# Last phase of a streaming encoder layer: the work on a tile's inputs given out at the end of a step

## The chip, the cores and the metric

The kernel runs on one core of one Trainium2 chip. The metric is the device time of one execution in microseconds (us). Before the change it is 2288.26 us, the median of three runs (2287.53 to 2289.09).

The core has five engines that each work through their own list of instructions in order: TensorE (PE in the profile; PEld is its loading of weights), VectorE (DVE), ScalarE (ACT), GpSimd (POOL), and SyncE (SP), which in this kernel issues the transfers. An instruction that waits holds back all that stand behind it on its engine.

## The reference, cut to what matters

One layer of an encoder with two token mixers side by side (differential attention A and stick-breaking attention B) is applied to 2048 new frames and to 8 running streams of 16 frames with 512 cached positions each. The phase that the change touches computes the end of the layer:

```
oa = rms_norm(oa, subln_g) * (1.0 - lam_init)
ya = (oa.reshape(b, s, WIDTH_A) * jax.nn.silu(za)) @ w_branch_a
yb = (ob.reshape(b, s, WIDTH_B) * jax.nn.silu(zb)) @ w_branch_b
y  = (jax.nn.sigmoid(ga) * ya + jax.nn.sigmoid(gb) * yb) @ w_out
x  = x + gate * y
out = rms_norm(x, final_g)
```

The widths are 512 for each branch and 1024 for the model. `oa` and `ob` together make the 1024 columns called o, `za` and `zb` those called z, `ga` and `gb` the 2048 columns of gates.

## The kernel before, in words

The rows are cut into 17 tiles of 128: 16 of the prompt, and one that holds all 8 x 16 rows of the running streams. The earlier phases project the inputs and compute both attentions, and leave o, z and gates of each tile in DRAM (`o_d`, `z_d`, `g_d`). The last phase takes the tiles in the order 0 to 14, then the tile of the running streams, then tile 15. All matrix products are made from numbers split in two 16-bit halves (`split`, lines 287 to 292): high by high, high by low, low by high.

For each tile the last phase does this:

- `inputs` (lines 1215 to 1246) loads o (L1218), z (L1219) and two halves of the gates (L1223). It makes u = o x z x sigmoid(z), scaled by the norm of each head for branch A: the sigmoid on ScalarE into a PSUM bank named "mm" (L1229, which shows in the profile as L120, the line of the helper `act`), o x z on GpSimd (L1230), and the product with the bank on VectorE (L1232 and four times L1236). It applies the sigmoid to the gates in place (L1238, again L120), takes the sum of squares of u (L274), and splits u into `u16`.
- `turned` (L1251) turns u16 by a transposing DMA, so that it can stand as weights of a matrix product.
- `branches` makes four pieces (two halves of columns for each of two branches) of 12 products of 128x128 by 128x512 each (L1262) into a bank "mm"; VectorE multiplies each with its gate (L1264), GpSimd adds the two branches (L1266). After the fourth, `finish` squares y and splits it into `y16`.
- `turned_y` (L1287) turns y16 by a transposing DMA.
- `output` makes two halves of 24 products each (L1399) into a bank "o", multiplies them with the gate of the layer (L1403; L1405 and L1406 for the running streams), adds x on GpSimd (L1407), and after the second half takes the norm of the row (L274, L255 to L266), scales it (L1412) and stores it (L1413). x is loaded at the first half (L1392).

Buffers: o, z and u16 have one buffer each (`hs`), the gates two tiles' worth, the turned u two, the turned y and y16 one. The banks "mm" and "o" are two each; "s" has three and "t" one.

The phase runs in steps n = 0 to 17 (L1439 to L1452). Step n makes the branches of the n-th tile in order, the output of the one before, and the inputs of the one two ahead. The list `work` of a step holds, in this order: two pieces of branches, the turn of u for the next tile, two pieces of branches, the inputs of tile n+2, two pieces of output of tile n-1, the turn of y of tile n. `interleave` spreads the steps of a second list (`aside`) through it: the attention of the running streams over their caches (`sample`; it loads caches at L753 and L758, transposes them at L777 and copies them at L778, and runs through steps 0 to 12), called the sample lane here. For the first two tiles `inputs` is called before this phase, in `early_work`.

The order of this list is a priority, not the final order: a scheduler places the instructions on each engine by their readiness in its own estimate of times, and gives out the banks in that order. A manual dependency of the kind NOSYNC orders two instructions of one engine without a wait. `act` uses it to keep the instructions that need an activation table in the order written.

Of the kernel before, what the change touches and what calls it, by code (L numbers as in the profile page):

```python
# [21 lines left out]
ALU = mybir.AluOpType  # L22
# [10 lines left out]
NT = SEQ // P  # L33
# [77 lines left out]
def layer_kernel(ctx: ExitStack, tc: tile.TileContext, a: dict):  # L111
    nc = tc.nc
    V, S, G, T = nc.vector, nc.scalar, nc.gpsimd, nc.tensor
# [1092 lines left out]
    L = {}  # L1206
# [5 lines left out]
        split(dst[:, 0, :, :], dst[:, 1, :, :], st, s, S if n % 2 else G)  # L1212
        return dst

    def inputs(t):

        o, z = hs[0:2]
        load(out=o, in_=o_d[t])  # L1218
        load(out=z, in_=z_d[t])  # L1219
        gs = []  # L1220
        for j in range(2):
            gs.append(L["g"][(2 * len(begun) + j) % 4].rearrange("p (b n) -> p b n", b=2))
            load(out=gs[j], in_=g_d[t].rearrange("p (b n) -> p b n", b=2)[:, :, j * 512 : (j + 1) * 512])  # L1223
        begun.append(t)
        r = L["orms"][:, 4 * t : 4 * t + 4] if t < NT else rsqrt(osums[:, NT, :], 4, P, tiny, "rA")
        for n in range(2):
            c = slice(n * 512, (n + 1) * 512)
            sg = bank("mm")
            act(out=sg, in_=z[:, c], func=AF.Sigmoid)  # L1229
            G.tensor_tensor(out=o[:, c], in0=o[:, c], in1=z[:, c], op=ALU.mult)  # L1230
            if n == 1:
                V.tensor_tensor(out=o[:, c], in0=o[:, c], in1=sg, op=ALU.mult)  # L1232
            else:
                for h in range(4):
                    c = slice(h * P, (h + 1) * P)
                    V.scalar_tensor_tensor(out=o[:, c], in0=sg[:, c], scalar=r[:, h : h + 1], in1=o[:, c], op0=ALU.mult, op1=ALU.mult)  # L1236
        for g in gs:
            act(out=g, in_=g, func=AF.Sigmoid)  # L1238
        acc = tiny.tile([P, 1], F32, tag="uacc", name="uacc")
        sum_squares(o, D, acc)  # L1240
        su = scales(acc, unit, "su")
        u16 = hs[2].bitcast(F16).rearrange("p (f n) -> p f n", f=2)
        split(u16[:, 0, :], u16[:, 1, :], o, su[:, 0:1], S)
        iu = unit.tile([P, 1], F32, tag="iu", name="iu")
        V.tensor_tensor(out=iu, in0=su[:, 1:2], in1=L["s"][0][:, 1:2], op=ALU.mult)
        return dict(u16=u16, u=L["u"][len(begun) % 2], iu=iu, g=gs)

    def turned(st):

        st["u"] = st["u"].bitcast(F16).rearrange("p (k n) -> p k n", n=P)  # L1250
        nc.sync.dma_start_transpose(out=st["u"], in_=st["u16"].rearrange("p f n -> p (f n)"))  # L1251
# [33 lines left out]
    def turned_y(st):  # L1285
        st["y"] = yT = L["y"].bitcast(F16).rearrange("p (k n) -> p k n", n=P)
        nc.sync.dma_start_transpose(out=yT, in_=st["y16"].rearrange("p f n -> p (f n)"))  # L1287
# [18 lines left out]
    def early_work():  # L1306


        free.extend(units[7]["bufs"])

        def first(t):
            if "orms" not in L:
                L["orms"] = rsqrt(osums[:, 0:NT, :].rearrange("p t h -> p (t h)"), 4 * NT, P, con, "orms")
            states[t] = inputs(t)
            if t == tiles[0]:
                turned(states[t])

        def early(i):

            if i == 0:  # L1320
                L["first"] = [fn for _, fn in branches(states[tiles[0]])] + [lambda: turned_y(states[tiles[0]])]
            L["first"][i]()

        def rest():
            L["g"], L["u"], (L["y"], L["y16"]) = free[0:4], free[4:6], free[6:8]

        return [branch_weight for _ in branch_weights] + [rest] + [lambda t=t: first(t) for t in tiles[0:2]] \
            + [lambda i=i: early(i) for i in range(5)]
# [31 lines left out]
    with ExitStack() as c2:  # L1360
        def pool2(name, bufs):
            return c2.enter_context(tc.tile_pool(name=name, bufs=bufs, reuse_waits="tile"))

        dec = pool2("dec", 1)
        res = pool2("res", 1)
        s2 = pool2("s2", 2)
        wb, (s_b, s_o) = L["wb"], L["s"]
        wo = []
        for j in range(2):
            for k in range(0, KT, 2):  # L1370
                st = s2.tile([P, D], F32, tag="x", name="x", bufs=2)
                wo.append(cut(res.tile([P, 2048], F16, name=f"wo{len(wo)}"), st, w_out, k, j, s_o[:, 0:1], k // 2))
        gate = res.tile([P, D], F32, name="gate")
        sel = res.tile([16, 256], F32, name="sel")
        load(out=sel, in_=a["shapes"][0:16, C_SEL : C_SEL + 256])
        fg = gts

        def gate_rows(i, n):

            pg = bank("t")  # L1380
            gsm = s2.tile([P, 512], F32, tag="sg", name="gsm", bufs=2)
            load(out=gsm[0:9, :], in_=gate_d[:, n * 512 : (n + 1) * 512])
            T.matmul(pg, sel[0:9, i * P : (i + 1) * P], gsm[0:9, :], start=True, stop=True)
            return pg

        def output(t, st):
            box = {}

            def half(j):
                if j == 0:  # L1390
                    box["x"] = s2.tile([P, D], F32, tag="x", name="x2", bufs=2)
                    load(out=box["x"], in_=x_rows(t))  # L1392
                x = box["x"]
                c = slice(j * 512, (j + 1) * 512)
                po = bank("o")
                n = 0
                for yi, wi in ((0, 0), (0, 1), (1, 0)):
                    for k in range(KT):
                        T.matmul(po, st["y"][:, yi * 8 + k, :], wo[j * 4 + k // 2][:, wi, k % 2, :], start=(n == 0), stop=(n == 3 * KT - 1))  # L1399
                        n += 1  # L1400
                m = s2.tile([P, 512], F32, tag="sg", name="m", bufs=2)
                if t < NT:
                    V.scalar_tensor_tensor(out=m, in0=po, scalar=st["iy"], in1=gate[:, c], op0=ALU.mult, op1=ALU.mult)  # L1403
                else:
                    S.activation(out=m, in_=po, func=AF.Identity, scale=st["iy"])  # L1405
                    V.tensor_tensor(out=m, in0=m, in1=gate_rows(1, j), op=ALU.mult)  # L1406
                G.tensor_tensor(out=x[:, c], in0=m, in1=x[:, c], op=ALU.add)  # L1407
                if j == 1:
                    acc = tiny.tile([P, 1], F32, tag="facc", name="facc")
                    sum_squares(x, D, acc)  # L1410
                    r = rsqrt_one(acc, D, tiny, "rF")
                    V.scalar_tensor_tensor(out=x, in0=x, scalar=r, in1=fg, op0=ALU.mult, op1=ALU.mult)  # L1412
                    load(out=y_rows(t), in_=x)  # L1413

            return [(5.2, lambda j=j: half(j)) for j in range(2)]

        fixed = [res.tile([P, NB, 32], F32, name="qz"), res.tile([P, 2, P], F32, name="qn"), res.tile([P, P], F32, name="kn"),
                 [res.tile([P, 4, NB, 32], F32, name=f"wz{c}") for c in range(2)], res.tile([P, 2, P], F32, name="wn")]
        for x in fixed[0:2] + fixed[3]:
            G.memset(x, 0.0)  # L1420

        lane = []
        for u in range(8):
            for i, pieces in enumerate(sample(units[u], dec, fixed)):
                if S_PERIOD * u + i == len(lane):
                    lane.append([])
                lane[S_PERIOD * u + i] += pieces

        def aside(n):

            m = -(-len(lane) // max(1, S_TILES - n))
            made = [piece for pieces in lane[:m] for piece in pieces]
            del lane[:m]
            return made

        for n in range(2):
            S.copy(out=gate[:, n * 512 : (n + 1) * 512], in_=gate_rows(0, n))
        load(out=fg, in_=a["final_g"].rearrange("(o d) -> o d", o=1).to_broadcast([P, D]))
        for n in range(NT + 2):  # L1439
            work = []  # L1440
            if 0 < n <= NT:
                work += branches(states[tiles[n]])
            if n + 1 <= NT:

                work.insert(2, (0.9, lambda n=n: turned(states[tiles[n + 1]])))
            if n + 2 <= NT:
                work.insert(5, (0.1, lambda n=n: states.update({tiles[n + 2]: inputs(tiles[n + 2])})))
            if n > 0:
                work += output(tiles[n - 1], states.pop(tiles[n - 1]))
            if 0 < n <= NT:  # L1450
                work.append((0.9, lambda n=n: turned_y(states[tiles[n]])))
            interleave(work, aside(n))  # L1452


# [25 lines left out]
```

## Time and profile before

| | us |
|---|---|
| median of the runs | 2288.26 |
| the profiled execution | 2285.48 |
| its span | 2283.7 |
| TensorE busy over the span | 2085.1 (91%) |
| VectorE busy | 1611.5 (71%) |
| ScalarE busy | 1482.6 (65%) |
| GpSimd busy | 688.1 (30%) |

The first output products (L1399) of the last phase start at 1790.6 us and the last at 2272.8 us. A line of the timeline gives start and length in us, the engine, the line of the kernel, the operation, what it writes and reads, the number of instructions merged, and in brackets the idle time of the engine before it with what ended it. The chain of waits gives start, length and what. A line of the busy time by stretches gives the stretch, its length, then busy time and number of instructions of PE, PEld, DVE, ACT and POOL, the granted TensorE clock as a share of the full one, the busy share of the DMA engines, and GB/s. A line of the table of waits gives who waited for whom: total us, times, longest. `hs` is the buffers of o, z and u16; `wa` and `wb` are buffers of many uses, here gates, turned u and y; `ps_mm`, `ps_o`, `ps_s`, `ps_t` are the banks.

### The profile page before, as it was taken

Reading aid. Unit: us, or ns where it says so; the run is one execution under the profiler, and the core shown is the slowest. Engines: PE = TensorE matmul, PEld = TensorE weight load, DVE = VectorE, ACT = ScalarE, POOL = GpSimd, SP = SyncE. Lnnn points to the kernel's source line nnn. Section 1 sums busy time; section 2 is a strip of 40 time slices with the busy share of each in tenths; the row PEclk is TensorE's granted clock in tenths of the full one; section 3 lists DMA queues with packets and bytes.
Section 4 is the critical chain, followed back from the end, with each engine's and each line's share of the span. In section 5 each row is a group of like instructions: output and inputs, shape, how many; then the busy total and the mean of one; then the engine's idle time right before and its main releaser. Section 6 shows DMA issues by size and latency. Waiting matters only on the chain. (4 is left out here: it accounts for less than half of the span.)

```text
span 2283.7 us, 40470 instructions
## 1 busy us (share of the span) xinstructions
PE 2085.1 (91%) x14478; PEld 1110.4 (49%) x14478; DVE 1611.5 (71%) x3507; ACT 1482.6 (65%) x2952; POOL 688.1 (30%) x559
## 2 busy tenths in 40 slices
PE   4997999999999999899999989999986799888997
PEld 2554554555555455455545555555543444444443
DVE  4668767789875778987577898776777656565554
ACT  3877677787876777786677777666776544444431
POOL 1522012355301335530032553012344232232321
PEclk7999999999999999999999999999997899999998
DMA  8667658697875778876566886757687989788652
GB/s 295 211 212 187 163 131 220 148 221 155 206 169 124 170 154 199 177 179 131 128 172 142 204 183 154 153 140 163 151 179 173 295 228 262 202 220 211 188 150 65
DMA packets 763754, 411.92 MB, mean 180 GB/s; under 512 B 524986, under 2 KB 708586, under 8 KB 763040
## 3 DMA queue, kind: packets, MB, share of 16 engines
q1 hardware_dynamic: 762474, 408.86, 72.6%
q8 instruction: 113, 1.85, 0.3%
q14 instruction: 89, 0.73, 0.1%
q10 hardware_dynamic: 1078, 0.48, 0.1%
HBM read 211.53 MB, written 72.91 MB: 125 GB/s over the span
## 5 line engine op out<-in xcount | busy, mean ns | idle before, releaser
L423 PE MATMUL ps_mm<-wb,hs 128*128 128x512 f16 x1836 | 460.7, 382 | 0.6 <-DVE v L292 0.5
L629 POOL TENSOR_TENSOR sc_p<-sc_p,sc_n 128x1024 f32<-128x1024 f32 (+8 forms) x160 | 278.1, 1742 | 459.2 <-DVE sc_n L607 451.6
L423 PEld LDWEIGHTS <-hs 128*128 128x128 f16 x2928 | 256.1, 98 | 226.9 <-issue 6.8
L607 DVE TENSOR_TENSOR_SCAN sc_n<-ps_s,sc_n,zero_t 128x512 f32<-128x512 f32 x192 | 245.3, 1278 | 64.4 <-ACT ps_s L120 62.2
L423 PE MATMUL ps_mm<-wa,hs 128*128 128x512 f16 x1092 | 279.4, 380 | 0.0
L647 PE MATMUL ps_s<-k,qst 128*128 128x512 f16 (+3 forms) x640 | 225.9, 354 | 38.3 <-DVE sc_n L607 30.1
L120 ACT ACTIVATE sc_p<-ps_s,usc 128x512 f32<-128x512 f32 (+3 forms) x320 | 202.0, 631 | 85.8 <-PE ps_s L648 55.1
L495 PE MATMUL ps_mm<-wa,hs 128*128 128x512 f16 x1020 | 257.0, 379 | 0.0
L562 DVE TENSOR_TENSOR sc_n<-sc_p,sc_n 128x1024 f16<-128x1024 f32 (+7 forms) x160 | 197.9, 1242 | 41.3 <-ACT sc_n L561 41.2
L648 PE MATMUL ps_s<-k,qst 128*128 128x512 f16 (+3 forms) x640 | 226.2, 354 | 0.0
L1399 PE MATMUL ps_o<-wo,wb 128*128 128x512 f16 x816 | 199.5, 401 | 24.7 <-DMA wb<-wa 22.0
L706 PE MATMUL ps_o<-v,wt 128*128 128x128 f16 x1008 | 175.6, 226 | 27.6 <-DMA wt<-sc_n 27.5
L495 PEld LDWEIGHTS <-hs 128*128 128x128 f16 x1632 | 140.2, 98 | 119.0
L120 ACT ACTIVATE ps_s<-ps_s,usc 128x512 f32<-128x512 f32 (+3 forms) x320 | 193.7, 605 | 0.0
L561 ACT CAST sc_n<-sc_p 128x1024 f16<-128x1024 f32 (+7 forms) x160 | 138.5, 870 | 49.2 <-POOL sc_p L629 49.1
L707 PE MATMUL ps_o<-v,wt 128*128 128x64 f16 x1008 | 158.5, 198 | 0.0
L495 PE MATMUL ps_mm<-wb,hs 128*128 128x512 f16 x612 | 155.9, 379 | 0.0
L706 PEld LDWEIGHTS <-wt 128*128 128x128 f16 x1008 | 99.2, 102 | 102.7 <-DMA wt<-sc_n 38.0
L1399 PEld LDWEIGHTS <-wb 128*128 128x128 f16 x816 | 82.1, 102 | 130.4 <-DMA wb<-wa 26.1
L457 POOL TENSOR_TENSOR rot<-pr,rope 128x256 f32<-128x256 f32 x68 | 63.1, 928 | 247.1 <-ACT pr L437 193.3
L437 ACT ACTIVATE pr<-ps_mm,usc 128x512 f32<-128x512 f32 (+1 forms) x136 | 86.5, 636 | 67.4 <-PE ps_mm L423 67.1
L545 DVE TENSOR_SCALAR_CACHE_REDUCE sc_n<-ps_s,usc 128x512 f32<-128x512 f32 (+3 forms) x148 | 99.0, 669 | 42.4 <-PE ps_s L648 28.2
(336 smaller groups left out, 4346.7 us busy)
## 6 DMA issues: line engine op xcount, KB each, us to landing
hs<-hT_d SPq DMA_DIRECT2D x122, 512.0 KB, 4.2
g_d<-gt SPq DMA_DIRECT2D x68, 256.0 KB, 3.4
out_dram<-pr SPq DMA_DIRECT2D x204, 64.0 KB, 1.8
wa<-g_d SPq DMA_DIRECT2D x25, 512.0 KB, 6.7
wide<-in_w_ada_dram SPq DMA_DIRECT2D x12, 1024.0 KB, 8.4
wa<-in_w_in_dram SPq DMA_DIRECT2D x44, 256.0 KB, 4.7
z_d<-pr SPq DMA_DIRECT2D x136, 64.0 KB, 2.7
o_d<-o SPq DMA_DIRECT2D x136, 64.0 KB, 2.7
```

The lines of the kernel that those rows point to most:

```text
L120: i = S.activation(**kw)
L423: T.matmul(box["p"], box["h"][:, hi, k, :], U["w"][k][:, wi, :], start=(n == 0), stop=(n == 3 * KT - 1))
L495: T.matmul(box["g"][:, 0:gw], box["h"][:, hi, k, :], U["wg"][k // per][:, k % per, wi, :], start=(j == 0), stop=(j == 3 * KT - 1))
L561: S.copy(out=hi, in_=src)
L562: V.tensor_tensor(out=lo, in0=src, in1=hi, op=ALU.subtract)
L607: V.tensor_tensor_scan(out=dst[:, lo : lo + n][:, ::-1], data0=src[:, 0:n][:, ::-1], data1=zero_t[:, 0:1].to_broadcast([P, n]), initial=fi ...
L629: G.tensor_tensor(out=p[:, 0:m], in0=p[:, 0:m], in1=n[:, 1 : m + 1], op=ALU.mult)
L647: T.matmul(p[:, 0:n], qst[:, c, :], kk[:, c, 0:n], start=True, stop=False)
L648: T.matmul(p[:, 0:n], qst[:, 2 + c, :], kk[:, c, 0:n], start=False, stop=not diag)
L706: T.matmul(po[:, c * P : (c + 1) * P], wt[:, wj, :], vt[:, c, :, :], start=first, stop=False)
L707: T.matmul(po[:, c * P : c * P + 64], wt[:, nb + wj, :], vt[:, c, 0, :], start=False, stop=last)
L1399: T.matmul(po, st["y"][:, yi * 8 + k, :], wo[j * 4 + k // 2][:, wi, k % 2, :], start=(n == 0), stop=(n == 3 * KT - 1))
```

## The change

`inputs` is cut in two. `started` does the loads and picks the buffers; it stands in the list where `inputs` stood. The rest, still called `inputs`, moves to the end of the step, behind the output pieces and the turn of y. Its product on GpSimd is ordered behind the last addition of x that was written before it (`L["added"]`), and its four products on VectorE behind the last scaling of x (`L["scaled"]`), both without a wait. The turn of u moves from between the second and third piece of branches to behind the fourth. The calls before the phase do both parts one after the other, as before.

```diff
-    def inputs(t):
+    def started(t):
 
         o, z = hs[0:2]
         load(out=o, in_=o_d[t])
...
         begun.append(t)
+        return dict(t=t, g=gs, u=L["u"][len(begun) % 2])
+
+    def inputs(st):
+
+        t, gs = st["t"], st["g"]
+        o, z = hs[0:2]
         r = L["orms"][:, 4 * t : 4 * t + 4] if t < NT else rsqrt(osums[:, NT, :], 4, P, tiny, "rA")
         for n in range(2):
             c = slice(n * 512, (n + 1) * 512)
             sg = bank("mm")
             act(out=sg, in_=z[:, c], func=AF.Sigmoid)
-            G.tensor_tensor(out=o[:, c], in0=o[:, c], in1=z[:, c], op=ALU.mult)
+            i = G.tensor_tensor(out=o[:, c], in0=o[:, c], in1=z[:, c], op=ALU.mult)
+            if "added" in L:
+                tc.add_manual_dep(i.ins, L["added"].ins.name, NOSYNC, reason="order of tiles")
             if n == 1:
                 V.tensor_tensor(out=o[:, c], in0=o[:, c], in1=sg, op=ALU.mult)
             else:
                 for h in range(4):
                     c = slice(h * P, (h + 1) * P)
-                    V.scalar_tensor_tensor(out=o[:, c], in0=sg[:, c], scalar=r[:, h : h + 1], in1=o[:, c], op0=ALU.mult, op1=ALU.mult)
+                    i = V.scalar_tensor_tensor(out=o[:, c], in0=sg[:, c], scalar=r[:, h : h + 1], in1=o[:, c], op0=ALU.mult, op1=ALU.mult)
+                    if "scaled" in L:
+                        tc.add_manual_dep(i.ins, L["scaled"].ins.name, NOSYNC, reason="order of tiles")
         for g in gs:
             act(out=g, in_=g, func=AF.Sigmoid)
...
-        return dict(u16=u16, u=L["u"][len(begun) % 2], iu=iu, g=gs)
+        st.update(u16=u16, iu=iu)
...
-            states[t] = inputs(t)
+            states[t] = started(t)
+            inputs(states[t])
...
-                G.tensor_tensor(out=x[:, c], in0=m, in1=x[:, c], op=ALU.add)
+                L["added"] = G.tensor_tensor(out=x[:, c], in0=m, in1=x[:, c], op=ALU.add)
...
-                    V.scalar_tensor_tensor(out=x, in0=x, scalar=r, in1=fg, op0=ALU.mult, op1=ALU.mult)
+                    L["scaled"] = V.scalar_tensor_tensor(out=x, in0=x, scalar=r, in1=fg, op0=ALU.mult, op1=ALU.mult)
...
             if n + 1 <= NT:
 
-                work.insert(2, (0.9, lambda n=n: turned(states[tiles[n + 1]])))
+                work.append((0.9, lambda n=n: turned(states[tiles[n + 1]])))
             if n + 2 <= NT:
-                work.insert(5, (0.1, lambda n=n: states.update({tiles[n + 2]: inputs(tiles[n + 2])})))
+                work.append((0.1, lambda n=n: states.update({tiles[n + 2]: started(tiles[n + 2])})))
             if n > 0:
                 work += output(tiles[n - 1], states.pop(tiles[n - 1]))
             if 0 < n <= NT:
                 work.append((0.9, lambda n=n: turned_y(states[tiles[n]])))
+            if n + 2 <= NT:
+                work.append((0.1, lambda n=n: inputs(states[tiles[n + 2]])))
             interleave(work, aside(n))
```

## The prediction

> **What bounds the kernel now.** I read the page first (span and slices), then the busy time by stretches, then TensorE's idle gaps in the timeline of the last phase, and last the chain of work and the waits behind these gaps.
>
> ```profile
> span 2283.7 us, 40470 instructions
> ```
>
> The profiled execution took 2285.48 us, 1.8 us more than its span and 2.8 us less than the median of the runs shown, 2288.26 us. The sum is made against 2285.48 and then laid on the median. The edited helper `inputs` is first called shortly before the last phase, but the order of the work changes only from 1800 us on. The next fence is the busy time by stretches: first nearly all of the edited phase, then 8 us behind one gap.
>
> ```profile
> 1815.00:2259.00 444.00, 401.99 (x2794) 204.11 (x2793) 250.72 (x676) 185.49 (x351) 126.25 (x95) 0.96 0.77 200
> 2000.00:2008.00 8.00, 7.74 (x28) 3.44 (x29) 5.64 (x19) 5.25 (x10) 2.73 (x2) 0.70 0.56 187
> ```
>
> TensorE is busy 402.0 of 444 us, VectorE 251, ScalarE 185, GpSimd 126: TensorE bounds the phase, and its 42.0 idle us, with the time at a lower clock behind them, are all that a new order can win. Now TensorE's larger gaps, from its timeline (the bracket has the idle time and its releaser):
>
> ```profile
> 1853.41 0.63 PE L777 MATMUL ps_s<-ident,dk 128*128 128x128 f32 x4 [2.91 <-DVE dsc L607]
> 2000.27 0.48 PE L818 MATMUL ps_t<-ident,dsc 128*128 128x128 f32 x1 [4.79 <-DVE dks L778]
> 2041.70 0.66 PE L777 MATMUL ps_s<-ident,dk 128*128 128x128 f32 x4 [2.26 <-DVE dsc L607]
> 2097.52 0.47 PE L818 MATMUL ps_t<-ident,dsc 128*128 128x128 f32 x1 [4.90 <-DVE dks L778]
> ```
>
> The named releasers are only the last link. The chain behind the gap at 2000 us, with the load that starts it:
>
> ```profile
> 1983.72 0.57 SPq L1218 DMA_DIRECT2D hs<-o_d  x1
> ```
> ```profile
> 1989.88 2.49 POOL hs L1230 x2
> 1992.36 1.23 POOL wa L1266
> ...
> 1995.65 0.61 ACT ps_mm L120
> ...
> 1996.34 1.14 DVE hs L1236 x4
> ...
> 1998.26 0.69 DVE hs L1232
> 1998.95 0.66 DVE wa L1264
> 1999.61 0.61 DVE dks L778
> ...
> 2000.27 0.48 PE ps_t L818
> 2000.74 7.06 PE ps_o L1399 x23
> ```
>
> GpSimd stands at the product of o and z for the tile after next (L1230) until o lands, 6.2 us after its issue. Behind it wait the sum of the present tile's branches (L1266), and in turn ScalarE and VectorE, which hold a sample copy (L778) that TensorE needs. The table of waits shows the same in total, and beside it ScalarE standing at the sigmoid of the gates until these land (the gap at 1853 us):
>
> ```profile
> POOL hs L1230 <- DMA hs<-o_d: 60.0, 8, 12.9
> ...
> ACT wa L120 <- DMA wa<-g_d: 51.6, 21, 7.0
> ```
>
> **What the change takes away.** The loads stay where they are in the order of the work (behind the four branch products). What is done on them moves behind both output halves of tile n-1 and the turn of y. Two ties hold it there: L1230 may not be placed on GpSimd before the last L1407, nor L1236 on VectorE before the last L1412. So L1266 of the present tile no longer stands behind a load, and ScalarE meets the gates late, when they have long landed.
>
> The output products' group, from the groups by line in the same stretch, and one run of them from the chain:
>
> ```profile
> L1399 PE MATMUL ps_o<-wo,wb 128*128 128x512 f16 x724 | 172.5, 392 | 15.9 <-DMA wb<-wa 15.9
> ```
> ```profile
> 2246.56 7.99 PE ps_o L1399 x37
> ```
>
> So 15.9 of the 42.0 us are waits for the turned y and 26.1 others. Of the others I take 21: the four gaps above alone are 14.9, and some sample copies will still come late. Of the waits for y I take 9: y's chain begins at L1266, but the tail, where no inputs are left, keeps its wait. At a steady 7.99/37 = 0.216 us, the 23 products after the gap at 2000 us would take 4.97 us and took 7.06; the clock was 0.70 there, and 0.96 over the stretch. Each such gap thus costs 2.1 us more, and I take 6 us for three of them. Gain: 21 + 9 + 6 = 36 us. Bounds: 15 us, if only the four gaps go, and 42 + 10 = 52 us, if all goes with the slow clock behind five gaps.
>
> [...]
>
> **What the move brings: a PSUM bank held longer.** `inputs` takes two banks named "mm" for the sigmoids of z, the same two that the branch products use. A bank is given back only when L1236 or L1232 has read it. In the timeline of before, the sigmoids run as soon as z and a bank are there, far ahead of their readers:
>
> ```profile
> 1800.36 1.10 ACT L120 ACTIVATE ps_mm<-hs 128x512 f32<-128x512 f32 x2
> 1806.57 3.40 POOL L1230 TENSOR_TENSOR hs<-hs,hs 128x512 f32<-128x512 f32 x2 [1.66 <-DMA hs<-o_d]
> 1810.90 0.68 DVE L1232 TENSOR_TENSOR hs<-hs,ps_mm 128x512 f32<-128x512 f32 x1
> ```
> ```profile
> 1760.20 0.60 ACT L120 ACTIVATE ps_mm<-hs 128x512 f32<-128x512 f32 x1 [1.21 <-DVE wa L1264]
> ...
> 1763.58 1.13 DVE L1236 SCALAR_TENSOR_TENSOR hs<-ps_mm,orms,hs 128x128 f32<-128x128 f32 x4 [3.41 <-POOL hs L1230]
> ...
> 1765.42 0.59 PE L1262 MATMUL ps_mm<-wa,wa 128*128 128x512 f16 x2 [2.08 <-DVE wa L1264]
> ```
>
> At 1800 us both banks are held for about 10 us, harmlessly, since TensorE is at the output products. At 1760 us a bank is held for 4.5 us while branch products want it, and TensorE idles for 2.08. After the change the sigmoids can still run early (only L1230 and L1236 are tied, and z's buffer comes free early), but their readers come after the last output half. The next thing that TensorE has to do then is the next tile's branch products, which need these banks. The delay is read from the last tile, where nothing else runs:
>
> ```profile
> 2273.32 0.75 DVE L1403 SCALAR_TENSOR_TENSOR m<-ps_o,iy,gate 128x512 f32<-128x512 f32 x1 [0.41 <-PE ps_o L1399]
> ...
> 2274.15 1.26 POOL L1407 TENSOR_TENSOR x<-m,x 128x512 f32<-128x512 f32 x1 [3.08 <-DVE rF L266]
> ```
>
> From the last product: 0.41 us to L1403, 0.83 from its start to L1407's, 1.26 for that, 2.49 for the two L1230, 0.69 for L1232, which carries no tie and frees the first bank: 5.7 us. Tiles 3 to 16 of the order go through it, in steps 1 to 14: 14 x 5.7 = 80 us.
>
> What can fill it is the sample lane, in steps 1 to 12. Its transposes come in groups of four:
>
> ```profile
> 2007.80 0.44 PE ps_t L777 x4
> ```
>
> Two cache buffers hold four such groups, 1.8 us; with 0.8 us for other lane pieces I take 2.6 us a gap, 31 us in all. The ends are 0 and 5.7 a gap. In steps 13 and 14 there is no lane, and two bare gaps cost 2.1 us each for the clock. Cost: 80 - 31 + 4 = 53 us. Were the bank free in time, this would be 0.
>
> [...]
>
> **What else moves.** The turn of u (L1251) goes behind the last two branch products. Those issue no DMA, so on SP's queue it passes only loads of the sample lane, and it stands ahead of the loads of o, z and gates as before.
>
> ```profile
> wb<-hs SPq DMA_TRANSPOSE x8, 7.1
> ```
>
> It lands 7.1 us after issue. With u16 made 13 us behind the last output half (the delay above, then squares, scales and splits), it lands some 14 us into the next branch products, and its reader comes one output group (48 x 0.216 = 10.4 us) and one gap later: cost 0, hidden by the output products, up to 7 us a step without them. The inputs' work passes L1392, L1413 and L1287 on SP's queue, but issues no DMA there. On ScalarE and VectorE it now runs beside the next branch products, and both have over 40% free. Where a wait was added, L1407 and L1266 of the next tile stand behind L1230 on GpSimd; its o was loaded some 10 us before: 0, at most the 6.2 us of a load.
>
> **Sum.** -36 + 53 = +17 us: 2302.5 us for the profiled execution, 2305 us on the median.
>
> **The rivals.**
>
> *The banks don't bind* (faster). If the lane fills every gap of steps 1 to 12, the cost is 80 - 68 + 4 = 16, and the change gives -20 us, 2268. If the sigmoids come so late that they find no waiting product behind them, it gives -36, 2252. For it: the chain of waits shows clearly what is taken away, and the lane has about (402 - 2 x 724 x 0.216 - 10)/11 = 7 us of TensorE work a step. Against it: both sigmoids at 1800 us. I put it at 2260.
>
> *It cancels.* A fill of 4.0 us a gap makes cost and gain meet: 80 - 48 + 4 = 36. The same holds if the placing of instructions, which follows readiness as the early sigmoids show, leaves things much as they were: 2288.
>
> *The sigmoid takes a bank ahead of the present tile's last branch product* (much slower). That is possible if z lands within the first two of the four products. Then the fourth waits until after the output half, y comes late too, and a gap of up to 5.7 + 4 us opens each step: 14 x 4 = 56 us more, 2360.
>
> **How the numbers follow.** The forecast's case has 0.46 (2292 to 2330: fills of 3.6 down to about 1.3 us a gap with the clock behind some), the banks not binding 0.34, cancelling 0.13, much slower 0.07. What a measurement of this kernel can tell from no change is 0.2%, 4.6 us. So faster 0.34, same 0.13, slower 0.53. Since both signs hold much, the range reaches from 2260 to 2332; it leaves out the much slower case and some 0.13 of the faster one.
>
> **What would show it.** Right: L1230 with next to no wait for o; ScalarE's waits for the gates near zero; TensorE's gaps regular, one a step, just before L1262, with L1232, L1236 or L1264 as releaser, and sigmoids of z (L120, hs) several us ahead of L1236. Wrong: no gap before L1262, or sigmoids that run only just before L1236; then the time falls below 2280. If the gaps stand before L1399 with the turned y as releaser, the y chain is what I misjudged.

## The result, and the profile after

The changed kernel takes 2336.57 us (median of four runs, 2334.02 to 2339.42), against 2287.9 us for the kernel before: a ratio of 1.022, 95% interval 1.0207 to 1.0233. It is slower by 49 us where 17 were forecast; the range ended at 2332. The profiled execution took 2334.02 us, and its page begins so:

```profile
span 2332.2 us, 40465 instructions
...
PE 2105.9 (90%) x14478; PEld 1113.6 (48%) x14478; DVE 1620.3 (69%) x3507; ACT 1484.3 (64%) x2952; POOL 685.5 (29%) x559
```

The lines of the code have shifted: in the changed kernel L1236 is the product of o and z, L1240 and L1244 are its two kinds of readers on VectorE, L1272 the branch products, L1274 their product with the gate, L1276 the sum of the branches, L1410 the output products, L1418 the addition of x, L1423 its scaling, L1261 and L1297 the two turns.

The busy time of the edited phase, from 1815 us to the start of the last tile's output, which comes at 2307 us now and came at 2259 us before:

```profile
1815.00:2307.00 492.00, 418.86 (x2785) 205.00 (x2783) 260.76 (x684) 189.10 (x356) 127.25 (x97) 0.93 0.69 181
```

The stretch is 48 us longer, which is the whole loss. TensorE is idle for 492.0 - 418.9 = 73.1 us where it was 42.0, and busy for 16.9 us more with nearly the same work (2785 instructions on record for 2794); the granted clock fell from 0.96 to 0.93.

What was to be taken away is gone. The product of o and z on GpSimd (its instructions, then what they waited for) no longer waits for any load, where it stood 58.4 us before:

```profile
L1236 POOL TENSOR_TENSOR hs<-hs,hs x28: 1259/1275/1849, 1817.4 to 2256.3; 128x512 f32<-128x512 f32 x28
...
its engine sat idle before it (us, times) until:
who waited for it (us, times):
```

What has come is the held bank. One step from the timeline, between the last branch product of one tile and the first of the next (L1274 takes that last product out of its bank):

```profile
2219.66 0.60 ACT L120 ACTIVATE ps_mm<-hs 128x512 f32<-128x512 f32 x1 [3.48 <-DVE wa L1274]
2221.47 0.75 DVE L1274 SCALAR_TENSOR_TENSOR wa<-ps_mm,iu,wa 128x512 f32<-128x512 f32 x1 [1.84 <-PE ps_mm L1272]
2222.25 0.60 ACT L120 ACTIVATE ps_mm<-hs 128x512 f32<-128x512 f32 x1 [1.99 <-DVE wa L1274]
...
2225.25 2.51 POOL L1236 TENSOR_TENSOR hs<-hs,hs 128x512 f32<-128x512 f32 x2
...
2229.08 0.67 DVE L1240 TENSOR_TENSOR hs<-hs,ps_mm 128x512 f32<-128x512 f32 x1
...
2229.80 1.01 PE L1272 MATMUL ps_mm<-wa,wb 128*128 128x512 f16 x2 [6.65 <-DVE hs L1240]
...
2231.95 1.12 DVE L1244 SCALAR_TENSOR_TENSOR hs<-ps_mm,rA,hs 128x128 f32<-128x128 f32 x4
```

Both sigmoids run as soon as a branch product is out of its bank. The second one's reader, L1240, comes 6.8 us after it, behind the last output half; the first one's, L1244, comes 12.3 us after it. TensorE stands for 6.65 us until L1240 has given a bank back. Not every gap names L1240. Where a piece of the sample lane was placed into the gap, the gap stands before that piece and names what the piece waited for:

```profile
2004.72 1.11 PE L777 MATMUL ps_s<-ident,dk 128*128 128x128 f32 x4 [5.50 <-DVE rF L258]
2005.99 1.01 PE L1272 MATMUL ps_mm<-wa,wa 128*128 128x512 f16 x2 [0.16 <-DVE hs L1240]
```

The second new cost is y. The table of waits of TensorE (who waited for whom: total us, times, longest), from 1800 to 2333 us:

```profile
PE ps_o L1410 <- DMA wb<-wa: 28.7, 8, 6.1
PE ps_mm L1272 <- DVE hs L1240: 9.3, 5, 6.6
```

The output products waited 15.9 us for the turned y before and wait 28.7 us now, 3.3 us of each at the last tile. The banks themselves are named for only 9.3 us, and for 3.5 us more before a branch product that waits for L1274. So this table alone doesn't show that the rest of the 73.1 us hangs on the banks; that is left to the experiments. For y the timeline shows how, here behind the last branch product of one tile (after, then before):

```profile
2242.50 0.60 ACT L120 ACTIVATE ps_mm<-hs 128x512 f32<-128x512 f32 x1 [1.02 <-DVE wa L1274]
...
2244.83 8.15 PE L1410 MATMUL ps_o<-wo,wb 128*128 128x512 f16 x37
2245.82 0.60 ACT L120 ACTIVATE ps_mm<-hs 128x512 f32<-128x512 f32 x1 [2.71 <-DVE wa L1274]
...
2259.03 0.68 DVE L1240 TENSOR_TENSOR hs<-hs,ps_mm 128x512 f32<-128x512 f32 x1
2259.07 6.25 PE L1410 MATMUL ps_o<-wo,wb 128*128 128x512 f16 x22 [6.09 <-DMA wb<-wa]
...
2265.15 0.59 PE L1272 MATMUL ps_mm<-wa,wa 128*128 128x512 f16 x2
```
```profile
2199.50 8.15 PE L1399 MATMUL ps_o<-wo,wb 128*128 128x512 f16 x37
2207.48 0.59 PE L1262 MATMUL ps_mm<-wa,wa 128*128 128x512 f16 x2
...
2219.01 4.05 PE L1399 MATMUL ps_o<-wo,wb 128*128 128x512 f16 x11 [2.90 <-DMA wb<-wa]
```

While y is squared, split and turned, TensorE does the 37 output products that are left of the tile before. In the kernel before it then goes on with the next tile's branch products, and 2.90 us of waiting are left. In the changed kernel the two sigmoids hold both banks until 2259 us and later, so these branch products can't start, and the wait is 6.09 us. Counted so for the last 15 tiles, every tile before but the last (which has no next) had 24 to 48 branch products of the next tile ahead of its own output. In the change five had none besides the last, and these are the five whose output waited more than 2 us for y, 23.3 us in all. The fourth branch product itself isn't later behind the first: the four take 15.6 us on average, and took 16.1.

### The profile page after: what moved, and what is told of

Its sections match the earlier page's. It is cut to its first block, busy times and chain, and to the rows that moved or that the text cites. A ratio compares the mean times of both kernels' runs of the same rounds, so it can differ in the third digit from the quotient of the medians.

```text
span 2332.2 us, 40465 instructions
## 1 busy us (share of the span) xinstructions
PE 2105.9 (90%) x14478; PEld 1113.6 (48%) x14478; DVE 1620.3 (69%) x3507; ACT 1484.3 (64%) x2952; POOL 685.5 (29%) x559
## 4 chain that ended last, share of the span: by engine, by line
PE 58%; DVE 13%; DMA 11%; ACT 7%; issue 6%; POOL 3%; SPq 1%; POOLq 0%; ACTq 0%; DVEq 0%
PE ps_mm L423 18%; PE ps_mm L495 12%; PE ps_mm L1272 7%; PE ps_o L1410 6%; DMA wt<-sc_n 5%; PE ps_s L647 3%; PE ps_s L648 3%; DVE sc_n L607 3%; DMA wb<-wa 2%; PE ps_o L706 1%; DVE wb L292 1%; ACT junk L274 1%; ACT sc_p L120 1%; POOL sc_p L629 1%; DVE wa L292 1%
## 5 line engine op out<-in xcount | busy, mean ns | idle before, releaser
L120 ACT ACTIVATE sc_p<-ps_s,usc 128x512 f32<-128x512 f32 (+3 forms) x320 | 202.2, 632 | 85.7 <-PE ps_s L648 56.8
L1410 PE MATMUL ps_o<-wo,wb 128*128 128x512 f16 x816 | 202.8, 404 | 39.5 <-DMA wb<-wa 35.9
L120 ACT ACTIVATE ps_s<-ps_s,usc 128x512 f32<-128x512 f32 (+3 forms) x320 | 194.0, 606 | 0.0
L1410 PEld LDWEIGHTS <-wb 128*128 128x128 f16 x816 | 82.4, 103 | 150.2 <-DMA wb<-wa 40.0
L706 PEld LDWEIGHTS <-wt 128*128 128x128 f16 x1008 | 100.1, 102 | 104.6 <-DMA wt<-sc_n 39.2
L707 PEld LDWEIGHTS <-wt 128*128 128x128 f16 x1008 | 97.9, 101 | 65.1 <-issue 3.3
```

Source lines behind the costliest of these rows:

```text
L120: i = S.activation(**kw)
L706: T.matmul(po[:, c * P : (c + 1) * P], wt[:, wj, :], vt[:, c, :, :], start=first, stop=False)
L707: T.matmul(po[:, c * P : c * P + 64], wt[:, nb + wj, :], vt[:, c, 0, :], start=False, stop=last)
```

## The experiments

All times are medians; the ratio is to runs of the kernel before on the same chip, with its 95% interval. Theory A is that of the forecast: the inputs' sigmoids hold the two banks "mm" until readers that now come late. B is that the work as such comes too late, and C that the turn of u does.

**No bank.** The changed kernel with the sigmoid written over z:

```diff
-            sg = bank("mm")
-            act(out=sg, in_=z[:, c], func=AF.Sigmoid)
             i = G.tensor_tensor(out=o[:, c], in0=o[:, c], in1=z[:, c], op=ALU.mult)
...
+            sg = z[:, c]
+            act(out=sg, in_=z[:, c], func=AF.Sigmoid)
```

> The changed kernel, but with the sigmoid of z written over z itself, behind the product of o and z, so that the inputs' work holds no bank named mm. Theory A (the two banks, held from an early sigmoid until readers that stand behind the last output half, take the branch products apart, delay y and leave gaps before L1272 and L1410): the branch products of a tile come in one piece again, idle time of TensorE in the phase falls from 73 us to 40 or less, and the time to 2260 to 2290 us. Theory B (the work itself comes too late at the end of a step, so that u, the gates or y are late, whatever holds the banks): the time stays at 2325 us or more. Theory C (the turn of u behind the branch products is what is late): also 2325 us or more.

Measured: 2261.47 us, ratio 0.9888 (0.9865 to 0.9911). Without the bank the change is a gain of 25 us. Its busy time, to the start of its last tile's output, and the waits of TensorE (to 2231 us, so that the last tile's 3.3 us are in):

```profile
1815.00:2230.00 415.00, 394.65 (x2845) 203.05 (x2843) 270.33 (x700) 194.36 (x364) 130.24 (x97) 0.99 0.87 225
```
```profile
PE ps_o L1410 <- DMA wb<-wa: 9.3, 6, 3.3
PE ps_mm L1272 <- DMA wa<-hs: 5.5, 1, 5.5
```

The idle time is 20.4 us and the clock 0.99. No branch product waits for a bank (the one wait, 5.5 us, is for the turned u), the turned y is late for 9.3 us in all, and each tile but the last again has 24 to 48 branch products of the next one ahead of its output. B and C fall here: the work and the turn of u are given out as late as in the change.

**The same edit in the kernel before.**

> The same edit in the kernel before, as a control: the sigmoid of z over z itself. Theory A: the bank was held only for 1 to 4 us there, so the time moves by at most 8 us from 2288. Theories B and C say the same.

Measured: 2289.48 us, ratio 1.0014 (1.0004 to 1.0025). Where the readers come early the bank costs nothing, so the 25 us above aren't a gain of the edit itself.

**No ties.** The changed kernel without both manual dependencies (the expectations call the reader L1242, as that run's lines have it; in the changed kernel it is L1244):

```diff
-            if "added" in L:
-                tc.add_manual_dep(i.ins, L["added"].ins.name, NOSYNC, reason="order of tiles")
...
-                    if "scaled" in L:
-                        tc.add_manual_dep(i.ins, L["scaled"].ins.name, NOSYNC, reason="order of tiles")
```

> The changed kernel without the two ties (no order of L1236 behind L1418 and of L1242 behind L1423). Theory A: the readers of the banks can then run as soon as o has landed, the hold is short as before the change, and the time is 2280 to 2310 us, with GpSimd standing before the load of o again for some 60 us. Theory B: the list still gives the work out late, so little changes: 2325 us or more. Theory C: 2325 us or more.

Measured: 2286.07 us, ratio 1.0004 (0.9992 to 1.0015). As expected of A: the readers follow the load again, the hold is short, and the new cost and the gain are both gone. GpSimd stands before the load of o for 41.2 us from 1815 us on, less than the 60 expected and the 58.4 of the kernel before.

**The sigmoid late.** The changed kernel with the sigmoid ordered on ScalarE behind the squares of x of the last output half:

```diff
-            act(out=sg, in_=z[:, c], func=AF.Sigmoid)
+            i = act(out=sg, in_=z[:, c], func=AF.Sigmoid)
+            if "squared" in L:
+                tc.add_manual_dep(i.ins, L["squared"].ins.name, NOSYNC, reason="order of tiles")
...
-                    sum_squares(x, D, acc)
+                    L["squared"] = sum_squares(x, D, acc)
```

> The changed kernel with a third tie: the sigmoid of z is ordered on ScalarE behind the squares of x of the last output half, so that it can't take a bank early. Theory A: the banks are free when the next branch products come, the hold is some 5 us and beside them; the time falls to 2265 to 2300 us. Theory B: the work comes later still, 2335 us or more. Theory C: 2325 us or more.

Measured: 2338.77 us, ratio 1.0231 (1.0213 to 1.0249). A as I had put it missed by 39 us. The time alone lies where B and C had put it; against them stand the run without a bank and the ones with another bank and a later claim below. The same step from this run's timeline (L1277 takes the last branch product out of its bank, L1243 is the reader, L1275 a branch product):

```profile
2226.22 0.75 DVE L1277 SCALAR_TENSOR_TENSOR wa<-ps_mm,iu,wa 128x512 f32<-128x512 f32 x1 [1.84 <-PE ps_mm L1275]
...
2230.69 1.10 ACT L120 ACTIVATE ps_mm<-hs 128x512 f32<-128x512 f32 x2
...
2233.11 0.68 DVE L1243 TENSOR_TENSOR hs<-hs,ps_mm 128x512 f32<-128x512 f32 x1
2233.85 1.01 PE L1275 MATMUL ps_mm<-wa,wb 128*128 128x512 f16 x2 [7.02 <-DVE hs L1243]
```

Both banks are empty from 2226.97 to 2230.69 us, TensorE has nothing else to do, and still it waits for the reader of a sigmoid that has not begun. So it is not the early sigmoid that takes the bank: it goes to the sigmoid ahead of the branch product that is later in the list, whenever the sigmoid runs. That is how these two runs read; how the scheduler decides it is not shown by any run.

**The turn alone, and the work alone.** The kernel before with only the turn of u moved; the changed kernel with the turn put back to where it was:

```diff
-                work.insert(2, (0.9, lambda n=n: turned(states[tiles[n + 1]])))
+                work.append((0.9, lambda n=n: turned(states[tiles[n + 1]])))
```

> The kernel before with only the turn of u moved behind the fourth branch piece; the inputs' work stays ahead of the output halves. Theory A (the banks do it): the turn has slack, 2280 to 2296 us. Theory C (the turn behind the products costs by itself): more than 2296 us.

> The changed kernel with the turn of u put back between the second and third branch piece; only the inputs' work is given out late. Theory A: all of the loss is here, 2328 to 2345 us. Theory C: the loss goes with the turn, below 2310 us.

Measured: 2293.04 us, ratio 1.0022 (1.001 to 1.0035), and 2346.51 us, ratio 1.0249 (1.0223 to 1.0276). The turn alone costs 0.2%; the loss comes with the work. The second is a little above its expected range.

**No bank, and the turn in its old place.**

> The run without a bank for the sigmoid (2261.5 us), with the turn of u put back between the second and third branch piece. Theory A: the turn's place matters little, 2255 to 2268 us. Theory C: the turn's new place has a cost that shows once the bank is out of the way, below 2255 us.

Measured: 2257.09 us, ratio 0.9878 (0.9839 to 0.9916). The interval covers that of the run without a bank, so the place of the turn makes no difference that these runs can tell. This version beats the kernel before by 1.2% and the changed one by 79 us.

**Another bank.** One word of the changed kernel: the sigmoid takes banks of the output products.

```diff
-            sg = bank("mm")
+            sg = bank("o" if "added" in L else "mm")
```

> The changed kernel with the sigmoid of z in banks named o (those of the output products) in place of mm, from step 1 on. It is PSUM as before, held as long. The late tie on the sigmoid gained nothing (2338.8 us) although it ran 7 us later, so theory A now reads: the bank is given out in the order of the list, to the sigmoid ahead of the next branch products, whenever the sigmoid runs. Then the next claim on a bank o comes some 10 us later, behind the branch products, and the hold is hidden: 2255 to 2280 us. If it is the sigmoid's place in PSUM or ScalarE's order that costs, and not the claim on mm: 2320 us or more.

Measured: 2263.34 us, ratio 0.9896 (0.9875 to 0.9917).

```profile
1815.00:2236.00 421.00, 392.42 (x2808) 201.56 (x2805) 261.56 (x693) 190.57 (x358) 123.62 (x96) 0.97 0.82 213
```

The work, its place, the ties and the sigmoid in PSUM are those of the change; only whose bank is claimed differs. TensorE's idle time falls from 73.1 to 28.6 us. With the turn in its old place as well:

> The run with banks o for the sigmoid (2263.3 us) and the turn of u in its old place. Theory A: the turn's place matters little, 2255 to 2270 us. Theory C: 2255 us or less.

Measured: 2261.6 us, ratio 0.9892 (0.9868 to 0.9917), the same.

**Claiming later.** The changed kernel with the inputs' work still later in the list, behind the second branch piece of the next step:

```diff
-            if n + 2 <= NT:
-                work.append((0.1, lambda n=n: inputs(states[tiles[n + 2]])))
...
+            if 0 < n and n + 1 <= NT:
+                work.insert(2, (0.1, lambda n=n: inputs(states[tiles[n + 1]])))
```

> The changed kernel, with the inputs' work put into the list still later: behind the second branch piece of the next step, banks mm and both ties kept. Theory A: the next two branch products now have their banks first, and the readers come soon after, so the hold is short and the time 2265 to 2300 us, though the work is given out later than in the change. Theory B (lateness): 2335 us or more.

Measured: 2274.98 us, ratio 0.9943 (0.9921 to 0.9966). Later work, and yet 62 us less than the change: the order of the claims decides, not the lateness. The turned y is still late for 18.6 us here (1815 to 2250 us), so it doesn't reach the runs without the hold.

**One tie.** The changed kernel without the tie on VectorE:

> The changed kernel with the tie on GpSimd kept and the one on VectorE (L1242 behind L1423) taken off. Theory A, as it now reads (two banks mm are given to the sigmoids ahead of the next branch products, and come back only when the readers have run): the reader of the second half is free of this tie already, so the first bank comes back at the same time and only the second some 3 us sooner; part of the loss goes, 2305 to 2330 us. If the tie on VectorE is what costs: 2295 us or less. If it does nothing: 2330 us or more.

Measured: 2340.87 us, ratio 1.0235 (1.0212 to 1.0259). My range was missed: beside the other tie, this one does nothing. With the tie on GpSimd alone the loss is there, and without both (2286.07 us) it isn't, so the tie on GpSimd is what keeps the readers late.

**No bank and no ties.**

> The run without a bank and with the old place of the turn of u (2257.1 us), without both ties. If the gain comes from keeping GpSimd from standing before the load of o, the ties carry it, and GpSimd stands there again for 40 us or more: 2272 to 2290 us. If the place at the end of the list is enough: 2265 us or less.

Measured: 2309.17 us, ratio 1.0104 (1.008 to 1.0128), 19 us above the expected range. Its waits from 1815 us on (L1234 is the product of o and z, L120 on `hs` its sigmoid, L1242 the reader):

```profile
ACT hs L120 <- POOL hs L1234: 39.0, 17, 6.6
DVE hs L1242 <- ACT hs L120: 35.5, 9, 6.1
POOL hs L1234 <- DMA hs<-o_d: 33.2, 6, 9.4
```

GpSimd stands before the load of o again for 33 us, where 40 or more were expected, and since the sigmoid now follows the product, ScalarE and VectorE stand behind it. So the ties carry the gain where no bank is held, and one of them makes the loss where it is.

## Why the prediction was wrong

The direction and its cause were right: the banks. With the run without a bank as the dividing line, the sum can be checked term by term, in the stretches from 1815 us to the last tile's output (444 us before, 415 without the bank, 492 after).

*Gain, forecast 36 us.* It is 444 - 415 = 29: the idle time fell by 42.0 - 20.4 = 21.6 us (forecast 30), the busy time by 402.0 - 394.7 = 7.3 (forecast 6). In medians it is 25. I had let 9 us of the waits for y go; these fell from 15.9 to 9.3, by 6.6. The gain was thus forecast 7 us too high.

*Cost, forecast 53 us.* It is 492 - 415 = 77. The idle time of the gaps was forecast as 80 - 31 = 49 and is 73.1 - 20.4 = 52.7, which is near in sum but not in what it is made of (below). The failed step is the other term: "In steps 13 and 14 there is no lane, and two bare gaps cost 2.1 us each for the clock." I charged the clock 4 us; it is 418.9 - 394.7 = 24.2 us. These 20 us, the 4 of the gaps and the 7 of the gain are the 31 us between +17 and +48.

Why the clock cost so much more shows behind the gap at 2229.80 us:

```profile
2229.80 1.01 PE L1272 MATMUL ps_mm<-wa,wb 128*128 128x512 f16 x2 [6.65 <-DVE hs L1240]
2230.61 1.06 PE L1272 MATMUL ps_mm<-wb,wb 128*128 128x512 f16 x2
2231.46 1.06 PE L1272 MATMUL ps_mm<-wa,wb 128*128 128x512 f16 x2
```

Two products start every 0.85 us, where two took 0.43 in the 37 output products of before from 2246.56 us on (2 x 0.216 us, at a granted clock of 1.00). The stretch in which the clock was lowered, from the busy time by stretches (the clock is the third number from the end):

```profile
2227.65:2234.48 6.83, 4.67 (x12) 1.64 (x12) 5.24 (x15) 0.05 (x1) 0.10 (x1) 0.50 0.71 205
```

At half the clock these 4.67 us of busy time cost 2.3 us, so the 2.1 us for a long gap was well sized. But I had counted two such gaps, as if the sample lane kept the clock up in all other steps, and 24.2/2.1 is over eleven. From 1815 to 2307 us the trace has 14 stretches at a clock of 0.50 in which TensorE works, for 53.9 us in all; the run without a bank has two, with 5.3 us. Half of the difference is 24.3 us, so the clock accounts for the whole term. The clock was lowered as well at a gap with a lane piece at its end (0.50 from 2002.37 to 2009.20 us, at the 5.50 us one that ends at 2004.72 us) and behind waits for y (0.50 from 2258.37 to 2261.78 us, at the one of 6.09 us). Nor were all of these gaps long: the clock was 0.50 from 1934.11 to 1937.52 us, behind a gap of 2.81 us, and from 1893.15 to 1896.56 us, behind one of 1.83 us.

*Where the gaps stand.* I put all of them before the branch products and gave y a gain. In fact the waits for y are 28.7 us, against 9.3 without the bank, so 19 of the 52.7 us stand before output products and some 33 are left for all other gaps, where I had priced those before the branch products at 49. That the idle sum came so near is luck. My own sign for a misjudged y chain, gaps before the output products with the turned y as releaser, is met in part. It is not the third rival, to which I gave 0.07: there the fourth branch product is late and y with it, while here the branch products behind it are missing.

*The reason given for the hold.* "After the change the sigmoids can still run early" is true, and yet not the cause: starting nearly 4 us after the banks are empty, the sigmoid costs the same. The claim goes by the place in the list. The 5.7 us for the delay were a little low (6.65 and 7.02 measured in a step without a lane).

*What was right.* GpSimd's wait for o is zero. The next tile did lack banks, though their number was enough: with the same number and another claim, the run with another bank took 73 us less. The cost of 0 for the turn of u was nearly right: 5 us alone, and nothing that can be told where no bank is held. The forecast that ScalarE would hardly wait for the gates failed; from 1800 us on it waits as follows, 59 us in all, less than the 82 us of before but far from zero:

```profile
ACT wa L120 <- DMA wa<-g_d: 33.8, 13, 7.8
...
ACT wb L120 <- DMA wb<-g_d: 25.3, 6, 8.1
```

What stays open: how much of the idle time before branch products, lane pieces and output products hangs on each of the three alone, since taking the hold away changed them together, and why the version without bank and ties is 24 us slower than the kernel before.

## What to carry to other kernels

When work is moved later in a list, look at what it holds from its place in the list to its last reader, not only at its engines: a buffer claimed ahead of the next tile's work and given back behind the present tile's is a wait of one full chain in every step. Before the move is given up, let the held thing come from another pool, whose next claim lies behind work that covers the hold; here that one word was worth 73 us. And charge TensorE's idle gaps with the slow products behind them, which were 24 of the 77 us of cost here, also where small pieces of work were placed into the gap.
